# The up projection of a gated MLP by Strassen's seven block products, with the down projection as a stage of its own

## The chip, the core and the metric

The kernel runs on one core of a Trainium2 chip. The metric is device time in microseconds (us) of one execution; several executions are timed and their median is taken. A profile is one more execution, with every instruction recorded on its engine: TensorE (PE, with its weight loads as PEld), VectorE (DVE), ScalarE (ACT), GpSimd (POOL) and SyncE (SP, whose queue issues the DMAs here).

## What is computed

One encoder block: a retention mixer and a Mamba-2 mixer, gated and merged, then an output projection and a conv-gated MLP. 1024 tokens and 16 meta tokens, model width 1024, MLP width 2816. The change touches what follows the mixers:

```python
    merged = jax.nn.sigmoid(gate_ret) * y_ret + jax.nn.sigmoid(gate_ssd) * y_ssd
    h = h + merged @ w_out

    f = dw_conv_centred(rms_norm(h, norm_ffn_w) @ w_ffn_up, w_ffn_conv, b_ffn_conv)
    fg, fu = _split(f, (D_FF, D_FF))
    return h + (jax.nn.silu(fg) * fu) @ w_ffn_down
```

`dw_conv_centred` is a depthwise convolution over three neighbouring tokens. A last `rms_norm` follows and the meta tokens are dropped.

## The kernel before

Activations lie feature-major: 128 features on the partitions, tokens along the free dimension. Every dense product is split so that float32 precision is kept with TensorE's float32r matmuls: an operand x is carried as hi + lo, and a product is hi·hi + hi·lo + lo·hi, three matmuls for each 128 features of the contraction (`mm3`, lines 140 to 142). `wload` (lines 126 to 134) brings 512 KB of weights by DMA into one of two `wraw` buffers, ACT casts them to `whi`, DVE subtracts to get `wlo`; three of each are kept. `fm` makes a block: 8 x 3 matmuls into one bank of PSUM.

The code is written engine-neutral in one order; a scheduler then sets the order of each engine's instructions, and each engine runs its own queue in order.

Output projection (lines 996 to 1013): for each of three token blocks of 342 (`BLK_B`) and each of eight output tiles d, load `w_o[d]`, make the block, add the residual into `h2[d]`, and sum squares into `acc` on POOL. `norm2` turns a finished block into `u2h`, `u2l`, the normalized MLP input in two parts; the last block's `norm2` is called between products of the first feature tile.

MLP (from line 1016): `up_tile(j)` takes feature tile j of 22, which has a gate half and an up half. For each half it loads one weight tile, makes three blocks of 342 tokens, copies them out of PSUM on ACT (line 1033), and runs the convolution: one POOL instruction (line 1039) and two on DVE (lines 1040, 1041) over 1024 tokens. The gate half gets SiLU on ACT; DVE multiplies the halves (line 1065), and the result is split into `ah[j]`, `al[j]` (lines 1068, 1069), which stay in SBUF, six of each. The 22 tiles form six parts of four or three. When a part is done, the next part's first tile is made and then `down` multiplies the finished part with its weights, 512 tokens at a time, and DVE adds the products to `h2` in SBUF (line 1088). The down projection is thus woven into the up projection. `last_down` does the last part in blocks of 256 tokens together with the final norm and the output.

## Time and profile before

| | us |
|---|---|
| device time, median of 3 runs | 2515.85 (2509.86 to 2518.0) |
| span of the profiled execution | 2511.8 |
| PE busy in it | 2423.6 (96%) |
| DVE, ACT, POOL busy | 1179.7 (47%), 770.1 (31%), 671.4 (27%) |
| output projection, from 1660.4 to 1752.1 us | 91.7 |
| MLP without the last part of the down projection, 1752.1 to 2466.0 us | 713.9 |
| last part, 2466.0 to 2499.3 us | 33.3 |

The page gives no other time of the profiled execution than its span, which lies within the three runs and 4.0 us below their median. The rows below come from that execution. A row of a group gives line, engine, operation, output and inputs with their shapes, the count, the busy time, and the mean duration of one in ns; a row of a timeline gives start and duration in us, and in brackets how long the engine had been idle and what ended that. Durations of matmuls that follow each other overlap in such rows, so what one costs is read from the distance between starts.

### The profile page before, as it was taken

The page shows a single profiled execution, that of the slowest core. Times are in us where ns is not written, and L with a number is a line of the kernel's source. Part 1 is how long each engine was busy: PE and PEld are TensorE (multiplying, and loading weights), DVE is VectorE, ACT ScalarE, POOL GpSimd, SP SyncE. Part 2 cuts the span into 40 slices and gives each one's busy share as a digit, 9 for nine tenths or more (in the row PEclk, how much of TensorE's full clock was granted, in tenths as well). Part 3 has the DMA queues.
Part 4 walks back from the last instruction along what each step waited for, and adds up shares of the span by engine and source line. Part 5 has one row for each costly group of instructions (what it writes and reads, how often), then busy time and mean ns, then how long its engine had stood idle before and what let it go on. Part 6 is the DMA issues. An engine that isn't in the chain of part 4 may idle for free.

```text
span 2511.8 us, 36889 instructions
## 1 busy us (share of the span) xinstructions
PE 2423.6 (96%) x15114; PEld 2274.8 (91%) x15114; DVE 1179.7 (47%) x1595; ACT 770.1 (31%) x1345; POOL 671.4 (27%) x763
## 2 busy tenths in 40 slices
PE   7999999999899899989988999999999999999998
PEld 7999999998798889779888999999999989898997
DVE  6243343645634653563374442447543434444356
ACT  4312212333442542343233320235321212121224
POOL 2121221125514633651462122222110101010112
PEclk9999999999899999989999999999999999999999
DMA  4111112124722851572367643345111111111112
GB/s 145 53 47 43 51 47 62 56 80 145 172 72 100 183 115 55 162 169 55 102 192 151 202 141 101 96 134 167 50 51 42 51 44 49 51 43 51 43 43 76
DMA packets 125001, 231.70 MB, mean 92 GB/s; under 512 B 16608, under 2 KB 77536, under 8 KB 120736
## 3 DMA queue, kind: packets, MB, share of 16 engines
q1 hardware_dynamic: 124832, 229.34, 32.0%
q8 instruction: 119, 1.95, 0.3%
q14 instruction: 50, 0.41, 0.1%
HBM read 187.83 MB, written 41.47 MB: 91 GB/s over the span
## 4 chain that ended last, share of the span: by engine, by line
PE 79%; DMA 6%; DVE 5%; POOL 5%; ACT 3%; issue 2%; SPq 0%; DVEq 0%; POOLq 0%; ACTq 0%
PE psd L140 20%; PE psd L142 20%; PE psd L141 20%; PE psw L140 3%; PE psw L142 3%; PE psw L141 3%; DMA br<-row 3%; PE psy L436 2%; POOL t L822 1%; PE pss L397 1%; PE pss L751 1%; PE psb L772 1%; DMA yl<-yb 1%; DVE br L798 1%; DMA ka<-yr 1%
## 5 line engine op out<-in xcount | busy, mean ns | idle before, releaser
L140 PE MATMUL psd<-uh,whi 128*128 128x342 f32 (+3 forms) x1376 | 463.1, 337 | 7.2 <-ACT gs L285 7.2
L133 DVE TENSOR_TENSOR wlo<-wraw,whi 128x1024 fp32r<-128x1024 f32 (+2 forms) x196 | 250.7, 1279 | 453.1 <-ACT whi L132 452.9
L141 PE MATMUL psd<-ul,whi 128*128 128x342 f32 (+3 forms) x1376 | 443.6, 322 | 0.0
L142 PE MATMUL psd<-uh,wlo 128*128 128x342 f32 (+3 forms) x1376 | 443.0, 322 | 0.0
L132 ACT CAST whi<-wraw 128x1024 fp32r<-128x1024 f32 (+2 forms) x196 | 203.6, 1041 | 605.3 <-PE psd L141 398.2
L141 PE MATMUL psd<-u2l,whi 128*128 128x342 f32 x1056 | 337.1, 319 | 0.1
L142 PE MATMUL psd<-u2h,wlo 128*128 128x342 f32 x1056 | 336.2, 319 | 0.0
L140 PE MATMUL psd<-u2h,whi 128*128 128x342 f32 x1056 | 336.0, 318 | 0.0
L140 PEld LDWEIGHTS psd<-uh,whi 128*128 128x128 f32 (+1 forms) x1376 | 261.7, 190 | 16.8 <-issue 7.9
L141 PEld LDWEIGHTS psd<-ul,whi 128*128 128x128 f32 (+1 forms) x1376 | 261.0, 190 | 7.2 <-issue 6.8
L142 PEld LDWEIGHTS psd<-uh,wlo 128*128 128x128 f32 (+1 forms) x1376 | 260.5, 189 | 0.1
L140 PE MATMUL psd<-whi,uh 128*128 128x256 f32 x768 | 234.0, 305 | 0.4 <-ACT uh L213 0.4
L142 PE MATMUL psd<-whi,ul 128*128 128x256 f32 x768 | 217.2, 283 | 3.2 <-POOL ul L215 2.7
L141 PE MATMUL psd<-wlo,uh 128*128 128x256 f32 x768 | 217.2, 283 | 0.0
L1039 POOL TENSOR_SCALAR fo<-fraw,vec 128x1024 f32<-128x1024 f32 x44 | 83.4, 1896 | 471.4 <-ACT fraw L1033 471.4
L141 PEld LDWEIGHTS psd<-u2l,whi 128*128 128x128 f32 x1056 | 198.6, 188 | 0.9 <-DVE u2l L993 0.4
L140 PEld LDWEIGHTS psd<-u2h,whi 128*128 128x128 f32 x1056 | 198.9, 188 | 0.3
L142 PEld LDWEIGHTS psd<-u2h,wlo 128*128 128x128 f32 x1056 | 199.1, 189 | 0.0
L140 PEld LDWEIGHTS psd<-whi,uh 128*128 128x128 f32 x768 | 146.5, 191 | 11.5 <-issue 8.9
L141 PEld LDWEIGHTS psd<-wlo,uh 128*128 128x128 f32 x768 | 147.0, 191 | 5.9 <-issue 5.3
L142 PEld LDWEIGHTS psd<-whi,ul 128*128 128x128 f32 x768 | 146.3, 191 | 4.0 <-POOL ul L215 3.1
L140 PE MATMUL psw<-ah,whi 128*128 128x512 f32 (+1 forms) x400 | 149.1, 373 | 0.0
(239 smaller groups left out, 4628.1 us busy)
## 6 DMA issues: line engine op xcount, KB each, us to landing
br<-row SPq DMA_DIRECT2D x32, 1024.0 KB
wraw<-in_w_up SPq DMA_DIRECT2D x44, 512.0 KB
gt<-gate SPq DMA_DIRECT2D x72, 171.0 KB
wraw<-in_w_xbc SPq DMA_DIRECT2D x24, 512.0 KB
wraw<-in_w_o SPq DMA_DIRECT2D x24, 512.0 KB
wraw<-in_w_dn SPq DMA_DIRECT2D x19, 512.0 KB
gate<-gs SPq DMA_DIRECT2D x48, 171.0 KB
ka<-ys SPq DMA_DIRECT2D x32, 256.5 KB
```

The source lines that it names most:

```text
L132: nc.scalar.copy(hi[:, :n], raw[:, :n])
L133: nc.vector.tensor_sub(lo[:, :n], raw[:, :n], hi[:, :n].bitcast(F32))
L140: nc.tensor.matmul(ps, ah, bh, start=(i == 0), stop=False)
L141: nc.tensor.matmul(ps, ah, bl, start=False, stop=False)
L142: nc.tensor.matmul(ps, al, bh, start=False, stop=(i == n - 1))
L397: nc.tensor.matmul(ps[:, :256], st[("kd", d, c)][:n], vv(c), start=True, stop=True)
L436: nc.tensor.matmul(py[:n, :256], a, b, start=(i == 0), stop=(i == len(mms) - 1))
L751: nc.tensor.matmul(ps, bk(c), st[("xw", d, c)][:n], start=True, stop=True)
L772: nc.tensor.matmul(ps[:n, :], tk("ct", c - 1), st[("pb", c)], start=True, stop=True)
L798: nc.vector.tensor_tensor(r, r, tok[:n, c, 0, g * 16:g * 16 + 16].unsqueeze(2).broadcast_to([n, 16, n]), op=ALU.add)
L822: nc.gpsimd.tensor_tensor(hv(t1[:n]), hv(x), bc(cd[:n, 0:8], n), op=ALU.mult)
L1039: nc.gpsimd.tensor_scalar(o, raw[:, 2:2 + SEQ], V("fconv_w", 3 * f + 1), V("fconv_b", f), op0=ALU.mult, op1=ALU.add)
```

## The change

The up projection of one feature tile has 2 x 2 blocks: W's two halves of the contraction (512 features each) by gate and up half, and u's two halves of the contraction by two sets of tokens. Strassen's form (with Winograd's sums) makes that product from seven block products instead of eight. A block product here is 4 x 3 matmuls of 256 or 258 tokens. Tokens are taken in two rounds (`RND`), 0 to 511 and 512 to 1025, two blocks each.

- `norm2_steps` normalizes a round in place in `hb`, forms four sums and differences of its blocks (t1 to t4; three on POOL, one on DVE), and splits the seven operands `b11`, `t2`, `t1`, `t3`, `b21`, `t4`, `b22` into hi and lo, on ACT and DVE. Both rounds' operands stay in SBUF.
- `weights(j)` loads the gate and the up tile. Four POOL instructions of 512 columns turn the raw tiles into the four weight sums, in place, and ACT and DVE split seven blocks of 512 columns (as `a1`, `a2`, `s24`, `s31`). There are five buffers each for hi and lo, in two pools.
- `up_round` makes the seven products in four PSUM banks: `p2`, `p4` and `p3` accumulate on banks that held another product. Five additions on DVE and two copies on ACT combine them into `f`. All eight banks are used once in a feature tile.
- `conv_steps` is the convolution, now with the multiplication of the halves on POOL. The result goes to DRAM (`act_d`) instead of SBUF.
- The output projection runs in two rounds of 16 weight loads in all (before: three blocks, 24 loads). `h2` is also stored to DRAM (`h2_d`), since `hb` is used for other things in the MLP, and read back for the down projection.
- The down projection follows the last feature tile: `act_load` reads a tile of activations back and splits it on ACT and DVE.

The rest of the kernel is the same. The diff, cut to this; lines that only fell away (the old `norm2`, `up_tile` and their loops) are those of the code above:

```diff
+RND = [((0, 256), 256), ((512, 770), 258)]
+RB = [((0, 256), (256, 256)), ((512, 258), (770, 256))]
...
+    hb = hp.tile([P, KT, NB + 2], F32, name="hb")
...
+    def op_tiles(pool, r):
+        n = RND[r][1]
+        return {o: [pool.tile([P, 4, n], F32R, name=f"{o}{x}{r}", tag=f"{o}{x}") for x in "hl"] for o in OPS}
+    ops = [op_tiles(oa, 0), None]
...
+    def norm2_steps(r, acc):
+        t0 = RB[r][0][0]
+        m = RB[r][0][1] + RB[r][1][1]
+        n = RND[r][1]
+        u = [[hb[:, 4 * k:4 * k + 4, s:s + n] for s in RND[r][0]] for k in range(2)]
+        t1, t3, t2, t4 = u[0][0], u[0][1], u[1][1], u[1][0]
+        def put(o, src):
+            hi, lo = ops[r][o]
+            nc.scalar.copy(hi, src)
+            nc.vector.tensor_sub(lo, src, hi.bitcast(F32))
+        def scale():
+            for b0, bn in RB[r]:
+                ps = pm.tile([P, 512], F32, name="psn", tag="psm")
+                a = acc[:, b0 - t0:b0 - t0 + bn]
+                nc.tensor.matmul(ps[:, :bn], ones, a, start=True, stop=True)
+                nc.scalar.activation(a, ps[:, :bn], AF.Sqrt, bias=eps, scale=1.0 / D)
+                nc.vector.reciprocal(a, a)
+        def first():
+            for d in range(KT):
+                hs = hb[:, d, t0:t0 + m]
+                nc.vector.scalar_tensor_tensor(hs, hs, V("norm_ffn", d), acc[:, :m], op0=ALU.mult, op1=ALU.mult)
+                if d == 3:
+                    put("b11", u[0][0])
+            put("b22", u[1][1])
+            nc.gpsimd.tensor_sub(t1, u[0][1], u[0][0])
+            nc.gpsimd.tensor_sub(t3, u[1][1], u[0][1])
+            nc.vector.tensor_sub(t2, u[1][1], t1)
+            put("t2", t2)
+        def rest():
+            put("t1", t1)
+            put("t3", t3)
+            put("b21", u[1][0])
+            nc.gpsimd.tensor_sub(t4, u[1][0], t2)
+            put("t4", t4)
+        return [scale, first, rest]
...
+    for r in range(2):
+        t0 = RB[r][0][0]
+        m = RB[r][0][1] + RB[r][1][1]
+        acc = sg.tile([P, 516], F32, name="acc", tag="ka", bufs=3)
         for d in range(KT):
             hi, lo = wload(t["w_o"][d])
+            xr = wo.tile([P, 516], F32, name="xr", tag="xr")
+            nc.sync.dma_start(out=xr[:, :m], in_=t["xT"][:, d, T0 + t0:T0 + t0 + m])
+            hs = hb[:, d, t0:t0 + m]
+            for b0, bn in RB[r]:
+                ps = fm(hi, lo, mh, ml, KT, b0, bn)
+                sl = slice(b0 - t0, b0 - t0 + bn)
+                nc.vector.tensor_tensor(hs[:, sl], ps[:, :bn], xr[:, sl], op=ALU.add)
+            nc.sync.dma_start(out=h2_d[:, d, t0:t0 + m], in_=hs)
             if d == 0:
+                nc.scalar.activation(acc[:, :m], hs, AF.Square)
             else:
+                sq = wo.tile([P, 516], F32, name="sq2", tag="sq")
+                nc.scalar.activation(sq[:, :m], hs, AF.Square)
+                nc.gpsimd.tensor_tensor(acc[:, :m], acc[:, :m], sq[:, :m], op=ALU.add)
+            if d in (1, 2, 3) and pend is not None:
+                pend[d - 1]()
+        pend = norm2_steps(r, acc)
...
+    ops[1] = op_tiles(ob, 1)
+    nwt = [0]
+    def wsplit(src, n):
+        pool = wp if nwt[0] % 5 < 3 else wx
+        nwt[0] += 1
+        hi = pool.tile([P, 1024], F32R, name="whi", tag="whi", bufs=3 if pool is wp else 2)
+        lo = pool.tile([P, 1024], F32R, name="wlo", tag="wlo", bufs=3 if pool is wp else 2)
+        nc.scalar.copy(hi[:, :n], src)
+        nc.vector.tensor_sub(lo[:, :n], src, hi[:, :n].bitcast(F32))
+        return hi, lo
+    def weights(j):
+        w = {}
+        def load():
+            w["r"] = r = []
+            for half in range(2):
+                raw = wp.tile([P, 1024], F32, name="wraw", tag="wraw", bufs=2)
+                nc.sync.dma_start(out=raw, in_=t["w_up"][half * NF + j])
+                r.append(raw)
+            w["a1"] = wsplit(r[0], 1024)
+        def sums():
+            r = w["r"]
+            a11, a12, a21, a22 = r[0][:, :512], r[0][:, 512:], r[1][:, :512], r[1][:, 512:]
+            w["a2"] = wsplit(a22, 512)
+            nc.gpsimd.tensor_tensor(a22, a21, a22, op=ALU.add)
+            nc.gpsimd.tensor_sub(a21, a11, a21)
+            nc.gpsimd.tensor_sub(a11, a22, a11)
+            nc.gpsimd.tensor_sub(a12, a12, a11)
+        def s24():
+            w["s24"] = wsplit(w["r"][0], 1024)
+        def s31():
+            w["s31"] = wsplit(w["r"][1], 1024)
+        return w, [load, sums, s24, s31]
+    def product(ps, w, o, r, start):
+        key, half = {"b11": ("a1", 0), "b21": ("a1", 1), "t4": ("a2", 0), "t2": ("s24", 0), "b22": ("s24", 1),
+                     "t3": ("s31", 0), "t1": ("s31", 1)}[o]
+        hi, lo = w[key]
+        xh, xl = ops[r][o]
+        n = RND[r][1]
+        for k in range(4):
+            c = slice(half * 512 + k * P, half * 512 + (k + 1) * P)
+            for i, (a, b) in enumerate(((hi, xh), (hi, xl), (lo, xh))):
+                nc.tensor.matmul(ps[:, :n], a[:, c], b[:, k, :], start=start and k + i == 0, stop=k == 3 and i == 2,
+                                 skip_group_check=True)
+    def up_round(w, f, r):
+        n = RND[r][1]
+        a, b = RND[r][0]
+        m = RB[r][1][1]
+        x = f[0][:, b:b + n]
+        st = {}
+        def bank(pool, tag):
+            return pool.tile([P, 512], F32, name="psu", tag=tag)
+        def p1():
+            st[1] = bank(pm, "psm")
+            product(st[1], w, "b11", r, True)
+            nc.scalar.copy(x, st[1][:, :n])
+        def p6():
+            st[2] = bank(pd, "psd")
+            product(st[2], w, "t2", r, True)
+            nc.vector.tensor_tensor(x, st[2][:, :n], x, op=ALU.add)
+        def p5():
+            st[3] = bank(pd, "psd") if r else bank(pm, "psm")
+            product(st[3], w, "t1", r, True)
+        def p7():
+            st[4] = bank(pm, "psm")
+            product(st[4], w, "t3", r, True)
+            c = f[1][:, b:b + m]
+            nc.vector.tensor_tensor(c, st[4][:, :m], x[:, :m], op=ALU.add)
+            nc.vector.tensor_tensor(c, st[3][:, :m], c, op=ALU.add)
+        def p2():
+            product(st[1], w, "b21", r, False)
+            nc.scalar.copy(f[0][:, a:a + n], st[1][:, :n])
+        def p4():
+            product(st[4], w, "t4", r, False)
+            nc.vector.tensor_tensor(f[1][:, a:a + n], st[4][:, :n], x, op=ALU.add)
+        def p3():
+            product(st[3], w, "b22", r, False)
+            nc.vector.tensor_tensor(x[:, :m], st[3][:, :m], x[:, :m], op=ALU.add)
+        return [p1, p6, p5, p7, p2, p4, p3]
+    def conv_steps(j, f):
+        o = [hb[:, q, 0:SEQ] for q in (3, 4)]
+        def one(half):
+            fi = half * NF + j
+            raw = f[half]
+            nc.gpsimd.memset(raw[:, NB:NB + 1], 0.0)
+            nc.gpsimd.tensor_scalar(o[half], raw[:, 2:2 + SEQ], V("fconv_w", 3 * fi + 1), V("fconv_b", fi), op0=ALU.mult, op1=ALU.add)
+            nc.vector.scalar_tensor_tensor(o[half], raw[:, 1:1 + SEQ], V("fconv_w", 3 * fi), o[half], op0=ALU.mult, op1=ALU.add)
+            nc.vector.scalar_tensor_tensor(o[half], raw[:, 3:3 + SEQ], V("fconv_w", 3 * fi + 2), o[half], op0=ALU.mult, op1=ALU.add)
+            if half == 0:
+                nc.scalar.activation(o[0], o[0], AF.Silu)
+        def fin():
+            nc.gpsimd.tensor_tensor(o[0], o[0], o[1], op=ALU.mult)
+            nc.sync.dma_start(out=act_d[j], in_=o[0])
+        return [lambda: one(0), lambda: one(1), fin]
+    w, prep = weights(0)
+    for f_ in prep:
+        f_()
+    conv = [lambda: None] * 3
+    for j in range(NF):
+        nxt, prep = weights(j + 1) if j + 1 < NF else (None, [lambda: None] * 4)
+        f = [hb[:, q, :] for q in ((0, 1) if j % 2 == 0 else (5, 6))]
+        ra, rb_ = up_round(w, f, 0), up_round(w, f, 1)
+        if j == 0:
+            ra[0]()
+            ra[1]()
+            pend[0]()
+            ra[2]()
+            ra[3]()
+            pend[1]()
+            for p_ in ra[4:]:
+                p_()
+            pend[2]()
+            rb_[0]()
+            rb_[1]()
+        else:
+            for p_ in (ra[0], rb_[0], ra[1], rb_[1]):
+                p_()
+        prep[0]()
+        conv[0]()
+        for q in (2, 3):
+            if j:
+                ra[q]()
+            rb_[q]()
+        prep[1]()
+        conv[1]()
+        for q, g in ((4, prep[2]), (5, prep[3]), (6, conv[2])):
+            if j:
+                ra[q]()
+            rb_[q]()
+            g()
+        w = nxt
+        conv = conv_steps(j, f)
+    ROW = (2, 7, 0, 1, 5, 6, 3, 4)
...
+    def act_load(j):
+        raw = fp.tile([P, SEQ], F32, name="ar", tag="ar", bufs=4)
+        nc.sync.dma_start(out=raw, in_=act_d[j])
+        acth[j] = fp.tile([P, SEQ], F32R, name="ah", tag="ah", bufs=11)
+        actl[j] = fp.tile([P, SEQ], F32R, name="al", tag="al", bufs=11)
+        nc.scalar.copy(acth[j], raw)
+        nc.vector.tensor_sub(actl[j], raw, acth[j].bitcast(F32))
...
-    def down(pi):
+    def down(pi, nxt):
         p0, nk = PARTS[pi]
         for dd in range(4):
             hi, lo = wload(t["w_dn"][4 * pi + dd, :, :2 * nk * P], 2 * nk * P)
+            if dd < len(nxt):
+                act_load(nxt[dd])
...
+    for j in range(PARTS[0][1]):
+        act_load(j)
+    for c_ in conv:
+        c_()
+    for d in range(KT):
+        nc.sync.dma_start(out=hrow[d], in_=h2_d[:, d, 2:2 + SEQ])
+    for pi, (p0, nk) in enumerate(PARTS[:-1]):
+        q0, nq = PARTS[pi + 1]
+        down(pi, list(range(q0, q0 + nq)))
     last_down()
```

The order of instructions on the engines, at three places. First, DVE over one feature tile in the middle of the MLP. Before (`wlo` is the low part of a weight tile, lines 1040 and 1041 the convolution of a half, `al` the low part of the result):

```order
L133 TENSOR_TENSOR wlo_19083<-wraw_19080,whi_19082 128x1024
L1040 SCALAR_TENSOR_TENSOR fo_18889<-fraw_18809,vec_72,fo_18889 128x1024
L1041 SCALAR_TENSOR_TENSOR fo_18889<-fraw_18809,vec_72,fo_18889 128x1024
L133 TENSOR_TENSOR wlo_19178<-wraw_19175,whi_19177 128x1024
L1040 SCALAR_TENSOR_TENSOR fo_18980<-fraw_18900,vec_72,fo_18980 128x1024
L1041 SCALAR_TENSOR_TENSOR fo_18980<-fraw_18900,vec_72,fo_18980 128x1024
L1065 TENSOR_TENSOR fo_18889<-fo_18889,fo_18980 128x1024
L1069 TENSOR_TENSOR al_18986<-fo_18889,ah_18985 128x1024
```

In the changed kernel (line 1079 is the low part of a weight block, a2 of the next feature tile in the first row, then its s24 and s31; lines 1160 and 1164 are the additions of p4 and p3, line 1175 the convolution's first DVE instruction; in brackets the engines whose signals it waits for):

```order
L1079 TENSOR_TENSOR wlo_17836<-wraw_17768,whi_17835 128x512 [waits DMAHW6_49,PE_49,Activation_49]
L1160 TENSOR_TENSOR hb_12744<-psu_17805,hb_12744 128x256 [waits PE_49]
L1160 TENSOR_TENSOR hb_12744<-psu_17820,hb_12744 128x258 [waits PE_49]
L1164 TENSOR_TENSOR hb_12744<-psu_17779,hb_12744 128x256 [waits DVE_49,PE_49]
L1079 TENSOR_TENSOR wlo_17874<-wraw_17766,whi_17873 128x1024 [waits Activation_49]
L1164 TENSOR_TENSOR hb_12744<-psu_17792,hb_12744 128x256 [waits DVE_49,PE_49]
L1175 SCALAR_TENSOR_TENSOR hb_12744<-hb_12744,vec_72 128x1024 [waits Pool_49]
L1079 TENSOR_TENSOR wlo_17904<-wraw_17768,whi_17903 128x1024 [waits Activation_49]
```

And POOL there (lines 1098 to 1101 are the four weight sums, 1174 the convolution's first instruction, 1181 the multiplication):

```order
L1098 TENSOR_TENSOR wraw_17768<-wraw_17768 128x512 [waits DMAHW6_49,DVE_49,Pool_49]
L1099 TENSOR_TENSOR wraw_17768<-wraw_17766,wraw_17768 128x512 [waits DMAHW5_49,Pool_49]
L1100 TENSOR_TENSOR wraw_17766<-wraw_17768,wraw_17766 128x512 [waits Pool_49]
L1101 TENSOR_TENSOR wraw_17766<-wraw_17766 128x512 [waits Pool_49]
L1173 MEMSET hb_12744 128x1 [waits DVE_49]
L1174 TENSOR_SCALAR hb_12744<-hb_12744,vec_72 128x1024
...
L1181 TENSOR_TENSOR hb_12744<-hb_12744 128x1024 [waits Activation_49]
```

The weights of the next feature tile are now made from raw tiles through POOL, and the first of these steps, a2, waits for PE.

Second, PE at the first feature tile, where round 1 has just been normalized (operands end in h0, l0 for round 0 and h1, l1 for round 1; `whi_16723` belongs to the second feature tile):

```order
L1119 MATMUL psu_16691<-b11h1_16524,whi_16542 128x258 [waits Activation_49]
L1119 MATMUL psu_16691<-b11l1_16525,whi_16542 128x258 [waits DVE_49]
...
L1119 MATMUL psu_16740<-t3h1_16530,whi_16558 128x258 [waits Activation_49]
L1119 MATMUL psu_16810<-b11h0_15443,whi_16723 128x256
```

Ahead of these stand the 84 matmuls of the first tile's round 0, and behind them 31 matmuls of the second tile. Before, two blocks of each half stood there to cover the last `norm2`.

Third, DVE at the end of the up projection (`al` is the low part of an activation tile read back; line 1164 the last products' additions, 1175 and 1176 the last convolution):

```order
L1164 TENSOR_TENSOR hb_12744<-psu_21384,hb_12744 128x256 [waits PE_49]
L1176 SCALAR_TENSOR_TENSOR hb_12744<-hb_12744,vec_72 128x1024 [waits DVE_49]
L1175 SCALAR_TENSOR_TENSOR hb_12744<-hb_12744,vec_72 128x1024 [waits Pool_49]
L136 TENSOR_TENSOR wlo_21699<-wraw_21696,whi_21698 128x1024 [waits DMAHW2_49,Activation_49]
L1176 SCALAR_TENSOR_TENSOR hb_12744<-hb_12744,vec_72 128x1024 [waits DVE_49]
L1237 TENSOR_TENSOR al_21520<-ar_21517,ah_21519 128x1024 [waits DMAHW4_49,Activation_49]
L1237 TENSOR_TENSOR al_21526<-ar_21523,ah_21525 128x1024 [waits DMAHW5_49,Activation_49]
L1237 TENSOR_TENSOR al_21532<-ar_21529,ah_21531 128x1024 [waits DMAHW6_49,Activation_49]
L1237 TENSOR_TENSOR al_21538<-ar_21535,ah_21537 128x1024 [waits DMAHW7_49,Activation_49]
```

The first products of the down projection, which had blocks of the up projection ahead of them, now need these four.

## Rows read from the trace of the kernel before

**Rows 1.** Page, busy time of each engine, and granted clock in 40 slices
```profile
PE 2423.6 (96%) x15114; PEld 2274.8 (91%) x15114; DVE 1179.7 (47%) x1595; ACT 770.1 (31%) x1345; POOL 671.4 (27%) x763
PEclk9999999999899999989999999999999999999999
```
**Rows 2.** Stretches: length, busy us (instructions) of PE, PEld, DVE, ACT, POOL, clock, DMA
```profile
1660.40:1752.10 91.70, 91.70 (x580) 91.31 (x580) 59.72 (x82) 42.72 (x65) 23.29 (x19) 1.00 0.54 174
1752.10:2466.00 713.90, 713.76 (x4115) 671.35 (x4114) 312.14 (x299) 174.15 (x257) 92.60 (x92) 1.00 0.14 47
```
**Rows 3.** ACT's timeline, first block copied out in two feature tiles that follow
```profile
2058.24 0.44 ACT L1033 COPY fraw<-psd 128x342 f32<-128x342 f32 x1
...
2080.78 0.44 ACT L1033 COPY fraw<-psd 128x342 f32<-128x342 f32 x1
```
**Rows 4.** PE's timeline: matmuls of 256, then of 512 columns, first and last
```profile
2477.68 0.29 PE L140 MATMUL psw<-ah,whi 128*128 128x256 f32 x1
...
2483.09 0.28 PE L140 MATMUL psw<-ah,whi 128*128 128x256 f32 x1
2434.99 0.40 PE L140 MATMUL psw<-ah,whi 128*128 128x512 f32 x1
...
2444.79 0.40 PE L140 MATMUL psw<-ah,whi 128*128 128x512 f32 x1
```
**Rows 5.** Groups of ACT and DVE, shapes kept apart: count, busy us, mean ns
```profile
L132 ACT CAST whi<-wraw 128x1024 fp32r<-128x1024 f32 x191 | 199.7, 1047 | 596.0 <-PE psd L141 388.9 <-PE psw L141 145.6 <-PE psd L142 35.4
L926 ACT CAST krh<-ka 128x513 fp32r<-128x513 f32 x32 | 19.5, 622 | 43.0 <-DMA ys<-yt 12.6 <-DMA ka<-ys 12.4 <-DMA ka<-yr 10.5
L927 DVE TENSOR_TENSOR krl<-ka,krh 128x513 fp32r<-128x513 f32 x32 | 22.1, 712 | 39.8 <-ACT krh L926 39.7
L1040 DVE SCALAR_TENSOR_TENSOR fo<-fraw,vec,fo 128x1024 f32<-128x1024 f32 x44 | 56.5, 1285 | 48.5 <-POOL fo L1039 47.5 <-POOL fraw L1027 1.0
L1115 DVE TENSOR_TENSOR h<-psw,h 128x256 f32<-128x256 f32 x32 | 12.9, 414 | 2.9 <-PE psw L142 2.7
L991 DVE SCALAR_TENSOR_TENSOR uf<-h,vec,acc 128x342 f32<-128x342 f32 x24 | 13.0, 572 | 0.3
L1098 DVE RECIPROCAL acc<-acc 128x256 f32<-128x256 f32 x4 | 7.0, 1753 | 1.8 <-ACT acc L1097 1.8
L1097 ACT ACTIVATE acc<-psn,eps 128x256 f32<-128x256 f32 x4 | 1.9, 470 | 1.7 <-PE psn L1096 1.7
```
**Rows 6.** POOL by line: duration min/median/max in ns; last row as group
```profile
L744 POOL TENSOR_TENSOR xw<-x,tok x64: 1032/1043/2429, 547.1 to 1311.8; 128x512 f32<-128x512 f32 x60, 16x512 f32<-16x512 f32 x4
L835 POOL TENSOR_TENSOR t<-t,y x32: 1264/1282/1311, 608.1 to 1347.3; 128x512 f32<-128x512 f32 x32
L215 POOL TENSOR_TENSOR ul<-uf,uh 128x1024 fp32r<-128x1024 f32 x1 | 2.5, 2522 | 8.6 <-ACT uh L213 8.6
```
**Rows 7.** Timelines of DVE and POOL, where instructions of both meet, three times
```profile
2395.99 1.23 DVE L133 TENSOR_TENSOR wlo<-wraw,whi 128x1024 fp32r<-128x1024 f32 x1 [2.73 <-ACT whi L132]
2396.41 1.89 POOL L1039 TENSOR_SCALAR fo<-fraw,vec 128x1024 f32<-128x1024 f32 x1 [6.53 <-ACT fraw L1033]
2407.05 0.96 DVE L133 TENSOR_TENSOR wlo<-wraw,whi 128x768 fp32r<-128x768 f32 x1 [6.12 <-ACT whi L132]
2407.46 1.62 POOL L1039 TENSOR_SCALAR fo<-fraw,vec 128x1024 f32<-128x1024 f32 x1 [6.31 <-ACT fraw L1033]
1777.57 3.16 POOL L1039 TENSOR_SCALAR fo<-fraw,vec 128x1024 f32<-128x1024 f32 x1 [1.60 <-ACT fraw L1033]
1778.52 1.22 DVE L133 TENSOR_TENSOR wlo<-wraw,whi 128x1024 fp32r<-128x1024 f32 x1
```
**Rows 8.** PE's longest idle stretch, and PE and clock in stretches behind it
```profile
1371.70 0.65 PE L140 MATMUL psd<-uh,whi 128*128 128x342 f32 x1 [7.19 <-ACT gs L285]
1372.00:1376.00 4.00, 4.00 (x15) 4.00 (x15) 2.16 (x3) 1.62 (x3) 0.00 (x0) 0.50 0.81 256
```
**Rows 9.** A weight load of 512 KB: issue on SP, first use on ACT
```profile
1738.78 0.33 SPq L129 DMA_DIRECT2D wraw<-in_w_o  x1
1742.13 1.05 ACT L132 CAST whi<-wraw 128x1024 fp32r<-128x1024 f32 x1 [1.04 <-DMA wraw<-in_w_o]
```

117 lines of the change are left out of this document (24 added, 93 removed).

## The prediction, made before the changed kernel ran

> **What bounds the kernel now.** I read the page first: PE is busy 96% of the span at an almost always full clock [rows 1]. The table of stretches then shows the two stages that change: in the output projection and in the MLP, PE is busy in practically every microsecond, while DVE is busy 312 of 714 us, ACT 174 and POOL 93, and DMA moves at a share of 0.14 [rows 2]. So the time of this stage is the number of matmuls times the distance between their starts. Two feature tiles that follow each other begin 2080.78 - 2058.24 = 22.54 us apart [rows 3]; at 144 matmuls of 342 columns that is 0.1565 us for one. The change can gain only by fewer PE microseconds, and it can lose at each place where PE must now wait. Those places are searched below: the chain that makes the next tile's weights, the first tile, and the end of the up projection.
>
> **The matmuls of the up projection.** Two rounds of seven products of 12 matmuls make 168 in a tile instead of 144, each of 256 or 258 columns instead of 342. The trace has matmuls of 256 columns, each with a weight load of its own: 45 distances from 2477.68 to 2483.09, 0.1202 each; and of 512 columns: 42 distances from 2434.99 to 2444.79, 0.2333 each [rows 4]. Between 256 and 342 the distance grows by (0.1565 - 0.1202) / 86 = 0.00042 us for a column, so 258 columns cost 0.1210. A tile needs 84 x 0.1202 + 84 x 0.1210 = 20.26 us instead of 22.54: 2.28 less, and 22 tiles give **-50.2 us**. (Columns fall to 7/8, the time only to 0.90, since a part of each matmul doesn't shrink with the columns.) If the distance is off by 0.002, this term moves by 7 us.
>
> The Trainium skill (TensorE: Matmul & The Clock Gate, Back-to-back issue gap) gives an isolated matmul N/2.4 + 2.5 ns, so 109 ns for 256 columns and 145 for 342; by that the gain would be an estimated 22 x (144 x 0.145 - 168 x 0.1095) = 55 us. The trace has 120 and 156, and the measurement decides.
>
> **The output projection.** It becomes 576 matmuls of 256 and 192 of 258 columns, 576 x 0.1202 + 192 x 0.1210 = 92.5 us, instead of 576 of 342, 90.1: **+2.4**. That 8 of 24 weight loads go, and that the sums of squares move to fewer, longer instructions, is worth nothing: PE did not wait there [rows 2].
>
> **The wait in each feature tile.** Before, a tile's weights came ready through one ACT cast and one DVE subtraction, far ahead. Now the order shows a chain. The hi part of a2 of the next tile takes the buffer of the current tile's a1, so ACT waits for the last matmul of `b21` in round 1; call its issue T. Then come: 0.16 to the matmul's end, ACT's cast of 512 columns 0.62, DVE's lo part 0.71 [rows 5], then four POOL sums one after the other. POOL instructions of 512 columns took 1.04 with a second operand that is broadcast and 1.28 with two full ones, and 2.52 at 1024 [rows 6]; I take 1.28, 5.1 in all. Then ACT casts s24, 1.05, and DVE makes its lo part, 1.23: 8.9 in all, some 9.1 with hand-overs. Meanwhile PE has `t4` and `b22` in two rounds, and of the next tile `b11` in two rounds: six products, 72 matmuls, 8.7, then two matmuls of `t2` (hi·hi, hi·lo) before it needs the lo part: 8.9. So PE stands some 0.2 us in each tile if nothing meets the chain. What can meet it are a convolution's POOL instruction (some 1.1 alone) or its DVE instruction, 1.29 [rows 5], and the order puts both near it, so up to 1.3. I take 0.45 in each of 20 tiles, near the lower end since the waits before T leave the queues empty: **+9**; bounds 0 (sums of 1.04) and 26 (1.3 each).
>
> The engines beside the chain are no bound by themselves: in 20.3 us, POOL has 4 x 1.28 + 2 x 1.1 + 2.5 = 9.8 and DVE 3 x 1.23 + 0.71 + 4 x 1.29 = 9.5, beside ten PSUM additions of 0.41 [rows 5], 13.7 in all. The store and the reload of activations and h2 cost nothing on the path: 44 loads and stores of 512 KB in a stretch whose DMA share is 0.14 [rows 2], at 3.35 us from issue to use [rows 9] against 20 us of lead. Without that cover one load would cost those 3.35.
>
> **The first tile.** After the last block of the output projection come the addition 0.41 and the square on ACT, some 0.6, POOL's sum 1.28, the norm's matmul, Sqrt 0.47, two reciprocals of 256 columns, 1.75 each, six scalings of 512 columns (0.57 at 342, so some 0.77 each), two additions of 0.41 and b11's lo part, 1.2 [rows 5, 6]: 12.9. With a weight's lo part that the order puts ahead of the reciprocals, 1.23, and hand-overs, b11 is ready some 14.9 us after the last block. PE has the first tile's round 0, 84 matmuls less what stands ahead of the norm, and is through at about 11.5: it waits 3.4. Then round 1's `t3` needs POOL's t1 and t3, 2.5 each at 1024 elements [rows 6], the lo and hi parts, and comes at 22.5, where PE with b11, part of `t3` and nothing else in its order is through at 16.2: 6.3 more. The norm's matmul itself waits for POOL, 0.8. In sum 10.5. After its longest idle stretch of before, 7.19 us, the granted clock was 0.50, the level of 1.2 GHz, and 4.00 us held only 15 matmuls of 342 columns [rows 8], which at 0.1565 take 2.35: 1.7 lost. **+12.2**; bounds 6 (the waits overlap, full clock) and 18.
>
> **The end of the up projection.** Before, a finished part's `down` had a tile of the next part ahead of it. Now all of DVE's late work stands between the last product and the down projection: p3's addition 0.41, two of the convolution's instructions and one more, 1.29 each, a weight's lo part 1.23, and four lo parts of activations, 1.23 each [rows 5]. Summed, the fourth activation's lo part is ready at 10.4 us, with hand-overs and a POOL instruction in the convolution's chain up to 12.2; I take 11.2. PE's first 48 matmuls of 512 columns use all four; the order lets 20 of them come ahead of the fourth, the other 28 x 0.2333 = 6.5 come after it. Of 11.2 + 6.5 = 17.7 us, 48 x 0.2333 = 11.2 is work: 6.5 lost, with hand-overs 7, and 1.7 for the clock: **+8.7**; bounds 4 and 15.
>
> **The sum.** -50.2 + 2.4 + 9 + 12.2 + 8.7 = -17.9. The profiled execution's 2511.8 us of span becomes 2493.9; that span lies 4.0 below the median of the runs, 2515.85, so the median becomes **2498**.
>
> **Rivals.**
> (a) The covers hold: POOL's sums take 1.04, no instruction meets the chain, the first tile costs 6 and the end 4. -50.2 + 2.4 + 10 = -37.8: 2478. For it: POOL's 60 instructions at 1.04 [rows 6] and the small busy shares [rows 2]. Against: these had a broadcast operand.
> (b) One instruction of 1.1 to 1.3 meets the chain in every tile: +26 in place of +9, 2515, no change that shows. For it: the order puts the convolution's DVE instruction right between s24's and s31's lo parts.
> (c) Slower: DVE and POOL exclude each other. Where DVE's subtraction had begun 0.42 us before, POOL's instruction took 1.89 beside one of 1.23 and 1.62 beside one of 0.96, so it ends some 1.1 after DVE's end in both; beside two, 3.16 [rows 7]. If a POOL instruction of 1.1 and a DVE instruction of 1.29 both come into the chain in every tile, PE waits 2.4 a tile, 21 times: 50 in place of 9, 2539. It turns slower where the wait passes 26.9 / 21 = 1.28 us a tile. Against: during the four sums the order gives DVE mostly additions from PSUM, and POOL's 32 instructions with two full operands all took 1.26 to 1.31 [rows 6].
> The Trainium skill (SBUF — State Buffer, Who interferes with whom) states it as a rule: a DVE instruction with two inputs in SBUF contends with a GpSimd instruction that reads SBUF, and the second to issue blocks until the first is done. It speaks against this change, which gives POOL four sums a tile; the rows agree with it for POOL as the second, and no row shows how often it would strike.
> (d) The change doesn't bring what it says: a matmul of 256 columns, with banks changing and weights of its own, costs more than 0.134 us (22.54 / 168), and the saving is eaten; at 0.140 a tile takes 23.5, 22 x (23.5 - 20.26) = 71 more than in the sum, 2569. Against: the 45 distances of 0.1202, and weight loads there, too [rows 4].
>
> **How the numbers follow.** Forecast (2490 to 2508) 0.47, (a) 0.21, (b) 0.17, (c) 0.12, (d) 0.03. About 0.3%, 7.5 us, is what a measurement of this kernel can tell from no change. Forecast and (a) make faster, 0.68; (b) the same, 0.17; (c) and (d) slower, 0.15. The range reaches from a little below (a), with the first term 4 us better, to half way between (b) and (c): 2474 to 2530.
>
> **What would show it.** Starts of the up projection's matmuls 0.120 apart say the first term is right; 0.134 would kill the gain. Tiles 20.3 to 20.7 apart: the forecast; 21.5: (b); 22.6: (c). In the chain of waits, idle time of PE should end at s24's lo part (line 1079), at b11 and t3 of round 1 in the first tile, and at `al` ahead of the down projection, with a lower clock only behind the last two. The forecast is wrong if PE idles elsewhere, above all at DMA arrivals or at a PSUM bank that an addition has not freed, or if POOL's sums take 2 us or more.

## The result: slower, and where the time went

The changed kernel takes 2535.88 us (median of four runs, 2529.71 to 2537.23) where the kernel before takes 2515.07 in runs beside it: a ratio of 1.0084, 95% interval 1.0066 to 1.0103. It is 0.8% slower, some 21 us, and lies above the forecast (2498) and above its range (2474 to 2530). One execution of a later run, the one with the normalization in seven pieces, was a slow one (4961.14 us) and is left out of that run's time.

The page of the kernel after, busy time of each engine and granted clock in 40 slices, as in [rows 1]:

```profile
PE 2387.7 (94%) x15836; PEld 2230.3 (88%) x15836; DVE 1290.1 (51%) x1822; ACT 771.7 (31%) x1320; POOL 853.9 (34%) x873
PEclk9999999999899999999998999999899999999999
```

PE is busy 36 us less than before, so the change did take work off PE, but the span is 16.1 us longer (2527.9 against 2511.8): 52 us of new idle time. Idle time of PE is where it waits, so the question is where it waits now. Four stretches of the kernel after show in which stages, with the columns of [rows 2]: the output projection, the first two feature tiles, the next twenty, and the down projection up to its last part.

```profile
1658.15:1761.94 103.79, 96.16 (x774) 95.43 (x773) 57.50 (x67) 34.22 (x42) 32.81 (x18) 0.97 0.53 150
1761.94:1823.27 61.33, 44.07 (x296) 41.95 (x295) 44.40 (x45) 20.68 (x28) 24.50 (x19) 0.86 0.20 65
1823.27:2248.72 425.45, 409.04 (x3361) 403.60 (x3359) 269.54 (x362) 116.96 (x178) 230.07 (x179) 1.00 0.22 76
2254.47:2476.87 222.40, 215.50 (x914) 172.66 (x913) 107.38 (x128) 42.86 (x44) 7.72 (x2) 0.98 0.31 109
```

In each of them PE's busy time is now less than the length; before, the two were equal, but for 0.14 us of 714 in the MLP [rows 2]. A tile in which PE never waits takes 20.0 us: in the run without weight sums below, twenty tiles follow each other in 399.95 us, all of it PE time. With that price, and 168 matmuls a tile, so 0.119 each, the account of the two profiled executions is:

| us | measured | predicted |
|---|---|---|
| up projection's matmuls, 22 x (20.0 - 22.54) | -55.9 | -50.2 |
| output projection, 103.8 - 91.7 | +12.1 | +2.4 |
| first two tiles, 61.3 less 288 matmuls (34.3) | +27.0 | +12.2 |
| next twenty tiles, 425.4 - 400.0 | +25.4 | +9 |
| start of the down projection, 222.4 less 912 matmuls (212.8) | +9.6 | +8.7 |
| last part, from its first matmul to the end of the span, 51.0 - 49.5 | +1.5 | 0 |
| waits in the MLP of before that are gone; stages ahead of the change | -1.5; -2.2 | 0 |
| sum | +16 | -17.9 |

The saving came, and a little larger. What was mis-sized is the losses: the next four rows add to 74 us where 32 had been expected. PE's waits of the kernel after from the up projection to the start of the down projection, the four longest rows (what it waited for: us in total, times, longest):

```profile
PE psu L1119 <- ACT whi L1078: 15.4, 10, 5.7
PE psu L1119 <- DVE wlo L1079: 10.2, 15, 0.8
PE psw L143 <- ACT ah L1236: 5.9, 1, 5.9
PE psu L1119 <- ACT t3h L1008: 5.1, 1, 5.1
```

The first two rows are the product t2 with s24 (lines 1078 and 1079 are `wsplit`), the third is the first matmul of the down projection, the fourth round 1 of the first tile. The output projection has three waits of its own, PE's timeline there:

```profile
1732.50 0.39 PE L143 MATMUL psd<-mh,whi 128*128 128x256 f32 x1 [2.01 <-DVE hb L1052]
1744.08 0.48 PE L143 MATMUL psd<-mh,whi 128*128 128x256 f32 x1 [4.05 <-DVE hb L1052]
1750.53 0.39 PE L145 MATMUL psd<-mh,wlo 128*128 128x258 f32 x1 [1.57 <-DVE wlo L136]
```

A wait costs more than its length. The first two stretches below are one in full work and one right behind waits of 0.92 and 0.76 us at t2 in tile 16, followed by two matmuls of the second. The third stretch holds two waits of the same lengths in tile 11, followed by the matmul at which the second of them ended, and the next one:

```profile
2098.00:2104.00 6.00, 6.00 (x52) 6.00 (x51) 2.23 (x3) 1.94 (x3) 5.22 (x4) 1.00 0.23 90
2108.80:2113.00 4.20, 4.11 (x21) 4.11 (x22) 3.10 (x6) 1.14 (x2) 2.10 (x1) 0.59 0.38 125
...
2109.67 0.42 PE L1119 MATMUL psu<-t2l,whi 128*128 128x256 f32 x1
2109.88 0.41 PE L1119 MATMUL psu<-t2h,wlo 128*128 128x256 f32 x1
...
2000.50:2003.00 2.50, 1.21 (x8) 1.01 (x9) 1.99 (x4) 1.72 (x4) 0.61 (x1) 1.00 0.35 139
...
2002.29 0.38 PE L1119 MATMUL psu<-t2h,wlo 128*128 128x256 f32 x1 [0.76 <-DVE wlo L1079]
2002.51 0.28 PE L1119 MATMUL psu<-t2h,whi 128*128 128x256 f32 x1
```

In tile 16 the granted clock is 0.59 behind the waits, and the starts are 0.21 us apart instead of 0.12: the clock had gone to its lower level, 1.2 GHz, for 3.4 us. In tile 11 the granted clock stays 1.00, and only the matmul right behind each wait is slow, with 0.22 us to the next start.

Distances between starts, over their full price, give the shares. In the twenty tiles, distances above 0.45 us (the waits) add 20.1 us, the matmuls right behind a wait 3.6, and the lower clock of tile 16 1.5: together the 25.4 us within 0.2. (The rows of waits count from a matmul's modelled end and give 16.4 in these tiles.) In the first two tiles the lower clock costs 5.8 us, and in the output projection 3.0 beside 8.1 of waits.

### The profile page after: what moved, and what is told of

Read it like the earlier page. It is cut to its first block, busy times and chain, and to the rows that moved or that the text cites. A ratio compares the mean times of both kernels' runs of the same rounds, so it can differ in the third digit from the quotient of the medians.

```text
span 2527.9 us, 38787 instructions
## 1 busy us (share of the span) xinstructions
PE 2387.7 (94%) x15836; PEld 2230.3 (88%) x15836; DVE 1290.1 (51%) x1822; ACT 771.7 (31%) x1320; POOL 853.9 (34%) x873
## 5 line engine op out<-in xcount | busy, mean ns | idle before, releaser
L136 DVE TENSOR_TENSOR wlo<-wraw,whi 128x1024 fp32r<-128x1024 f32 (+1 forms) x144 | 190.5, 1323 | 217.1 <-ACT whi L135 216.8
L135 ACT CAST whi<-wraw 128x1024 fp32r<-128x1024 f32 (+1 forms) x144 | 149.3, 1039 | 482.7 <-PE psd L144 281.6
L1079 DVE TENSOR_TENSOR wlo<-wraw,whi 128x1024 fp32r<-128x1024 f32 x88 | 112.6, 1284 | 113.7 <-ACT whi L1078 113.6
L144 PE MATMUL psw<-al,whi 128*128 128x512 f32 (+1 forms) x400 | 149.0, 373 | 1.0 <-DVE al L1237 1.0
L145 PE MATMUL psw<-ah,wlo 128*128 128x512 f32 (+1 forms) x400 | 146.4, 367 | 0.0
L1078 ACT CAST whi<-wraw 128x1024 fp32r<-128x1024 f32 x88 | 81.5, 940 | 201.4 <-POOL wraw L1101 100.3
L143 PE MATMUL psd<-krh,whi 128*128 128x342 f32 x384 | 123.6, 322 | 3.2 <-ACT krh L932 3.2
L144 PE MATMUL psd<-krl,whi 128*128 128x342 f32 x384 | 123.7, 322 | 0.3 <-DVE krl L933 0.3
L145 PE MATMUL psd<-krh,wlo 128*128 128x342 f32 x384 | 123.4, 322 | 0.0
```

Of the source, the lines that this page charges most:

```text
L135: nc.scalar.copy(hi[:, :n], raw[:, :n])
L136: nc.vector.tensor_sub(lo[:, :n], raw[:, :n], hi[:, :n].bitcast(F32))
L143: nc.tensor.matmul(ps, ah, bh, start=(i == 0), stop=False)
L144: nc.tensor.matmul(ps, ah, bl, start=False, stop=False)
L145: nc.tensor.matmul(ps, al, bh, start=False, stop=(i == n - 1))
L1078: nc.scalar.copy(hi[:, :n], src)
```

## The experiments

Each run is given with its ratio to runs of the kernel before, taken beside it on the same chip; the kernel after stands at 1.0084. The diffs are against the kernel after.

### 1. Is it the chain behind a2, or POOL's sums themselves?

The four sums of tiles 2 to 22 written to free rows of `hb`, so that they need not wait for a2's split, which waits for a1's buffer:

```diff
-            w["a2"] = wsplit(a22, 512)
-            nc.gpsimd.tensor_tensor(a22, a21, a22, op=ALU.add)
-            nc.gpsimd.tensor_sub(a21, a11, a21)
-            nc.gpsimd.tensor_sub(a11, a22, a11)
-            nc.gpsimd.tensor_sub(a12, a12, a11)
+            if j == 0:
+                w["a2"] = wsplit(a22, 512)
+                s31_, s24_ = r[1], r[0]
+            else:
+                s24_, s31_ = hb[:, 2, :1024], hb[:, 7, :1024]
+            w["q"] = s24_, s31_
+            s3, s1, s2, s4 = s31_[:, :512], s31_[:, 512:], s24_[:, :512], s24_[:, 512:]
+            nc.gpsimd.tensor_tensor(s1, a21, a22, op=ALU.add)
+            nc.gpsimd.tensor_sub(s3, a11, a21)
+            nc.gpsimd.tensor_sub(s2, s1, a11)
+            nc.gpsimd.tensor_sub(s4, a12, s2)
+            if j:
+                w["a2"] = wsplit(a22, 512)
...
```

> The four weight sums of tiles 2 to 22 go to two rows of hb that are free by then, so they no longer wait for a2's split, which waits for a1's buffer. Theory 1 (the wait of PE at t2 is the length of the chain from a1's last matmul through a2 and four sums in a row): PE's idle time before the products of t2, 20 us over tiles 3 to 22 and 5.7 in tile 2, falls to under 5 in all, tiles come 20.3 us apart, and the kernel takes 2510 to 2518 us. Rival (DVE and POOL lock each other out, so that the sums cost their time wherever they stand): PE waits as long, 2529 to 2537 us.

Measured: 2503.43 us, ratio 0.9959 (0.9942 to 0.9976), 31 us below the kernel after. Twenty tiles take 403.3 us instead of 425.4, the first two 55.9 instead of 61.3. PE's waits in this run from tile 3 on are one row:

```profile
PE psu L1127 <- DVE hb L1159: 0.9, 3, 0.4
```

Theory 1 holds, and the gain is larger than it said: the tiles are back within 3.4 us of PE's own price, 400.0, and the granted clock is 1.00 in them. The rival falls, though not because DVE and POOL leave each other alone. POOL's timeline of this run, two of the four sums of one tile, and DVE's beside it:

```profile
2016.61 2.28 POOL L1105 TENSOR_TENSOR hb<-wraw 128x512 f32<-128x512 f32 x1
2018.85 2.28 POOL L1106 TENSOR_TENSOR hb<-hb,wraw 128x512 f32<-128x512 f32 x1
...
2015.44 2.29 DVE L1183 SCALAR_TENSOR_TENSOR hb<-hb,vec 128x1024 f32<-128x1024 f32 x1 [1.11 <-POOL hb L1182]
2017.66 2.31 DVE L1184 SCALAR_TENSOR_TENSOR hb<-hb,vec 128x1024 f32<-128x1024 f32 x1
```

The two engines take turns here, and each needs 2.3 us for what takes 1.28 alone, more than in the kernel after. It costs PE next to nothing, because its waits in these tiles are the 0.9 us above.

The sums left out (four lines deleted; s24 and s31 are split from the raw tiles, so other products are computed):

> The four weight sums are left out (s24 and s31 are split straight from the raw tiles; the products are then other ones). Theory 1: what it gains is what the run with spare rows gains, within 4 us, and 3 us more at the first tile, where the sums stand before the first t2: 2507 to 2516. Rival (POOL's work itself is the cost, by blocking DVE): it gains 20 us or more over the run with spare rows, which gains little.

Measured: 2489.47 us, ratio 0.9912 (0.9896 to 0.9929). That is 12 us below the run with spare rows by the ratios, more than theory 1 allowed and less than the rival: twenty tiles take 399.95 instead of 403.3, so the sums themselves cost 3 us there, and the first two tiles 48.7 instead of 55.9, where the sums of tile 1 stand ahead of the first t2 and those of tile 2 between the other work of this place.

The sums on DVE, in place, with the wait on a2 unchanged (`nc.gpsimd` to `nc.vector` in the four lines):

> The changed kernel with its four weight sums on DVE, in place as before, so that they still wait for a2's split and a1's buffer, and only their length changes (POOL 4 times 1.29 and a hand-over of 0.43 us, DVE 4 times 0.69, as seen with sums of the first tiles on DVE). Theory 1 (start plus length of the chain makes the wait at t2): the chain becomes some 2.5 us shorter than PE's cover needs, the idle time at t2 in tiles 3 to 22 falls from 20 to under 4 us, the first tiles win some 3 to 6, and the kernel takes 2507 to 2516. Rival (DVE is the engine that everything waits for, and gets 2.8 us more a tile): idle time goes over to other products, 2520 or more.

Measured: 2506.22 us, ratio 0.9982 (0.9969 to 0.9995). The twenty tiles take 409.0 us; PE's waits in them:

```profile
PE psu L1119 <- DVE wlo L1079: 6.1, 8, 0.8
```

So a shorter chain with the same start gains most of what an earlier start gains; 6.1 us of waits are left where under 4 were expected, and the time is just below what theory 1 gave. Start and length together make the wait at t2, and DVE, busy for 322 of the 409 us, is not short of time in these tiles.

### 2. The output projection

The normalization of round 0 in seven pieces behind output tiles 1 to 7 instead of three behind 1 to 3:

```diff
-            if d in (1, 2, 3) and pend is not None:
+            if d and pend is not None:
...
-        return [scale, first, rest]
+        return [scale, first, rest] if r else [scale, g1, g2, g3, g4, g5, g6]
```

> The normalization of round 0 is cut into seven pieces, put behind output tiles 1 to 7 of round 1 of the output projection instead of three behind tiles 1 to 3. Theory 1 (DVE's additions, which free PE's banks, queue behind 20 us of DVE work in three places): PE's idle time in this stage falls from 7.6 us to under 2, the stage from 103.8 to 94 or 95 us, the kernel to 2525 to 2529. Rival (the stage is long for its matmuls and its DMA, or DVE is slowed by POOL in any order): the stage stays above 101 us, 2533 to 2538.

Measured: the stage 97.9 us (103.8), PE's waits there 3.4 us (7.6). Theory 1 names the cause but not all of it. The whole time, 2529.24 us, ratio 1.0066 (1.0047 to 1.0085), is not clear of the kernel after: in the profiled execution the stages ahead take 2.8 us longer, and PE then waits 5.3 us instead of 3.6 for the first t2. What is left is a second cause. POOL's timeline in this run, then DVE's:

```profile
1731.87 2.39 POOL L1033 TENSOR_TENSOR hb<-hb 128x1024 f32<-128x1024 f32 x1 [4.08 <-DVE b11l L1009]
1734.22 1.75 POOL L1082 TENSOR_TENSOR acc<-acc,sq 128x514 f32<-128x514 f32 x1
...
1732.06 4.46 DVE L1022 SCALAR_TENSOR_TENSOR hb<-hb,vec,acc 128x512 f32<-128x512 f32 x2
1736.44 1.21 DVE L136 TENSOR_TENSOR wlo<-wraw,whi 128x1024 fp32r<-128x1024 f32 x1
```

Two scalings that take 0.74 us each elsewhere took 4.46 together: the first lasted until 0.55 us after the end of POOL's difference t1 (line 1033), the second until 0.55 after the end of POOL's next sum, and the weight's lo part, for which PE waits, stands behind them. So the differences were moved to DVE as well (lines 1026, 1027 and 1035, `nc.gpsimd` to `nc.vector`):

> As the run with the normalization in seven pieces, and the differences t1, t3 and t4 are made on DVE instead of POOL. Theory 2 (of what is left in the output projection, most is DVE blocked by POOL's instructions of 1024 elements, seen as subtractions that take 2.3 to 3.3 us instead of 1.2): the stage falls from 97.9 us to 95 or less and the kernel to 2523 to 2527, though DVE gets 3.7 us more work. Rival (DVE has too much work in this stage): the stage grows to 99 us or more, 2531 to 2536.

Measured: the stage 96.8 us, between the two theories; the whole time 2521.59 us, a little below theory 2; ratio 1.0049 (1.0028 to 1.0071). The rival falls, since more work on DVE did not lengthen the stage. Of theory 2 the larger part showed up behind the stage: from the start of the up projection to t4 of tile 2 it is 58.6 us instead of 62.9. What still stands in the stage are 2.4 us of waits for DVE and 1.5 of the lower clock.

### 3. The first tiles

The raw weights of tile 1 loaded right behind the last `w_o` tile:

> The two raw weight tiles of the first feature tile are loaded right behind the last tile of the output projection, ahead of its residual and its stores. Theory 1 (the first t2 waits for its loads): PE's idle time before the first t2 falls from 3.6 us to under 1.5, the kernel to 2530 to 2534. Rival (the four sums on POOL, in a row and between other work, set that time): 3 us or more are left, 2533 to 2538.

Measured: 2532.16 us, ratio 1.0078 (1.0061 to 1.0096), and PE waits 3.7 us before the first t2, as before. The time lies in the range of theory 1, but it is not clear of the kernel after, and the wait decides: the loads are not the cause; with the run without sums, in which this wait is gone, it is the four sums in a row.

Sums of the first two tiles and differences t1, t3, t4 on DVE and b21 ahead of t2 in round 1, on top of spare rows, seven pieces, buffers on the left (below) and the early load. First these four edits alone:

> Spare rows for the sums, the normalization in seven pieces, the buffers on the left and the early loads together. If the waits are in separate places, the gains add: 32 + 6 + 3 + 2 us from 2536, so 2491 to 2498. If what is gained in one place is waited for in the next (an earlier end of the output projection lets PE only wait longer in the first feature tile), 2498 to 2505.

Measured: 2495.93 us, ratio 0.9931 (0.9907 to 0.9954). The gains add as forecast, so the places are mostly separate. Then with the first tile:

> The four edits, and in the first feature tile the differences t1, t3, t4 and the weight sums of the first two tiles on DVE, and in round 1 the product of b21 (which needs no sum) ahead of that of t2. Theory 2 (POOL's 2.4 us for 1024 elements and its lock with DVE make the chain ahead of round 1 long): from the start of the up projection to t4 of the second tile 45 to 48 us instead of 56 to 61, and the kernel 6 to 10 us below the four edits alone. Rival (reciprocals and scalings on DVE alone set it, and DVE gets more work): within 3 us of the four edits.

Measured: 2489.48 us, ratio 0.9911 (0.9896 to 0.9925), and 51.2 us from the start of the up projection to t4 of tile 2 (58.7 with the four edits). The kernel is 6 us better, as theory 2 said, though the stretch is 3 us longer than it said. This version is 0.9% faster than the kernel before. PE still waits 5 us at the first matmul of t3 in round 1, while b21 is ready: the scheduler put that one matmul ahead of it. So t3 was made ahead of b21 (the diff's lines in `first`):

```diff
...
+            put("b22", u[1][1])
+            nc.vector.tensor_sub(t1, u[0][1], u[0][0])
+            nc.vector.tensor_sub(t3, u[1][1], u[0][1])
+            put("t3", t3)
+            put("b21", u[1][0])
...
```

> As the run with the first feature tile reworked, with t3 of round 1 made and split ahead of b21, t2 and t1, since one matmul of t3 stands first in PE's order there. If that matmul holds up 30 others that are ready: its wait falls from 5.0 us to 2.5 to 3.5, and the kernel comes 2 to 3 us below the run it is made from, 2486 to 2488. If what follows is late anyway: the wait moves to the next product, within 1 us of it.

Measured: 2491.68 us, ratio 0.9915 (0.9899 to 0.9932), no difference. PE's timeline of this run has the wait where it was:

```profile
1779.67 0.58 PE L1163 MATMUL psu<-t3h,whi 128*128 128x258 f32 x1 [4.60 <-ACT t3h L1008]
```

On DVE, b22's lo part still came ahead of the difference t3, and a wait of 0.85 us at t2 followed. Neither theory's number fits. The order of the run before shows that the one matmul holds up ready ones: b21's parts were there 3.4 us before it started. That moving it pays was not shown.

### 4. The start of the down projection

The buffers of the activations that are read back, over operands that are done with earlier:

```diff
+    ap = fp_es.enter_context(tc.tile_pool(name="ap", bufs=1, reuse_waits="tile"))
...
-        raw = fp.tile([P, SEQ], F32, name="ar", tag="ar", bufs=4)
+        raw = ap.tile([P, SEQ], F32, name="ar", tag="ar", bufs=4)
```

> The buffers of the activations that are read back lie over round 0's operands, which are done with earlier, instead of over operands of the last products. Theory 1 (PE's 5.9 us behind the last product are a wait for loads that are issued only after it): that idle time falls below 3 us and the kernel to 2530 to 2533. Rival (as predicted, DVE's queue of convolution and lo parts sets the time): the first matmul comes earlier, but the fourth lo part as late as before, and the down projection starts its steady run within 1.5 us of before: 2534 to 2537.

Measured: 2528.73 us, ratio 1.0068 (1.0051 to 1.0085), the down projection 220.9 us instead of 222.4. PE's first wait falls from 5.9 to 2.8 us, and 2.4 us come back two rows later at the first lo part (1.0 before). So theory 1 is right on the first wait and the rival on the stage, which is 1.5 us shorter; the whole time is below both and not clear of the kernel after. DVE's timeline behind the last product, which ended at 2258.19:

```profile
2262.52 1.28 DVE L1175 SCALAR_TENSOR_TENSOR hb<-hb,vec 128x1024 f32<-128x1024 f32 x1 [1.10 <-POOL hb L1174]
2263.72 2.35 DVE L1238 TENSOR_TENSOR al<-ar,ah 128x1024 fp32r<-128x1024 f32 x2
2265.99 1.28 DVE L1176 SCALAR_TENSOR_TENSOR hb<-hb,vec 128x1024 f32<-128x1024 f32 x1
2267.19 2.35 DVE L1238 TENSOR_TENSOR al<-ar,ah 128x1024 fp32r<-128x1024 f32 x2
```

The fourth lo part ends 11.4 us behind the last product's end, the predicted 11.2. To see whether DVE's queue alone sets this, the last tile's convolution was left out as well, on top of these buffers:

> As the run with the buffers on the left, and the convolution of the last feature tile is left out (its activation stored raw), which takes four DVE instructions of 1.28 us out from between the last product and the lo parts of the activations. If DVE's queue sets the start of the down projection, as predicted: the fourth lo part comes some 3 to 5 us earlier and the down projection takes 215 to 218 us instead of 220.9. If the loads set it (SP issues them late, each needs 1.3 us of DMA): 219 us or more.

Measured: 2532.47 us, ratio 1.0086 (1.0064 to 1.0107), the down projection 223.3 us. ACT's timeline of this run:

```profile
2250.32 1.05 ACT L135 CAST whi<-wraw 128x1024 fp32r<-128x1024 f32 x1 [2.38 <-PE psu L1119]
2258.12 1.04 ACT L135 CAST whi<-wraw 128x1024 fp32r<-128x1024 f32 x1 [6.75 <-DMA wraw<-in_w_dn]
2260.64 1.04 ACT L1237 CAST ah<-ar 128x1024 fp32r<-128x1024 f32 x1 [1.47 <-DMA ar<-act]
2261.90 1.04 ACT L1237 CAST ah<-ar 128x1024 fp32r<-128x1024 f32 x1 [0.22 <-DMA ar<-act]
```

The last product ends at 2253.11 here, and the first cast of a load comes 7.5 us behind it; with the convolution in place it came 1.9 us behind. SP's order changed with the edit: three more reads of h2 now stand ahead of the four loads, which are issued 0.6 us before the last product's end instead of 4.4. So in this run the loads set the start, and in the run before, where ACT had made the fourth hi part by 2264.93 and DVE its lo part by 2269.54, DVE's queue did. What the convolution costs by itself was not measured, and what either limit would leave without the other stays open.

## Why the prediction failed, step by step

The profiled execution is 34 us above the forecast's sum. By size, the terms that failed are the wait in each feature tile (16.4 us more than its term), the first tile (14.8) and the output projection (9.7); the matmuls give 5.7 back.

- **What bounds the kernel, the up projection's matmuls:** right. A tile has 7/8 of the block products, and they came at 0.119 us a matmul, 5.7 us better than summed. That a matmul of 256 columns would eat the saving (rival d) is refuted.
- **The output projection: the step that failed first in time.** It was costed as matmuls alone, +2.4 us, with "PE did not wait there" from the kernel before [rows 2]. But the change puts a whole round's normalization, with its sums and seven splits, into DVE's queue of this very stage, in three lumps. It measured +12.1, and the sign that the prediction had named itself, a PSUM bank that an addition has not freed. DVE's timeline between two of PE's waits, first and last rows, and POOL's beside the first:

```profile
1732.70 3.07 DVE L136 TENSOR_TENSOR wlo<-wraw,whi 128x1024 fp32r<-128x1024 f32 x1
1735.69 2.33 DVE L1009 TENSOR_TENSOR b22l<-hb,b22h 128x1024 fp32r<-128x1024 f32 x1
...
1742.48 1.22 DVE L1009 TENSOR_TENSOR t2l<-hb,t2h 128x1024 fp32r<-128x1024 f32 x1
1743.61 1.08 DVE L1052 TENSOR_TENSOR hb<-psd,xr 128x258 f32<-128x258 f32 x3
...
1732.25 2.43 POOL L1027 TENSOR_TENSOR hb<-hb 128x1024 f32<-128x1024 f32 x1 [0.69 <-DVE hb L1022]
```

  For 11 us DVE works on splits and a sum; then come three additions at once (line 1052), for which PE's banks had waited. It is not the amount of work: DVE is busy 57.5 us in this stage, and 59.7 before [rows 2]. It is that the pieces come in one lump, two of them lengthened by POOL, ahead of the additions: the run with seven pieces took 5.9 us off the stage. Nothing of this was costed: what is queued behind the moved work on its engine was asked for the MLP only.
- **The first tile:** 27.0 us against 12.2 and an upper bound of 18. The waits that were named came: 5.1 at t3 (6.3 forecast), 1.5 at b11 (3.4), 1.0 at the norm (0.8). The lower clock, put at 1.7, cost 5.8. Two waits were not named, both at t2, where the first tiles have the same chain of sums as all others but less work of other tiles to cover it:

```profile
1767.09 0.39 PE L1119 MATMUL psu<-t2h,whi 128*128 128x256 f32 x1 [3.56 <-ACT whi L1078]
...
1812.97 0.58 PE L1119 MATMUL psu<-t2h,whi 128*128 128x256 f32 x1 [5.65 <-ACT whi L1078]
```

- **The wait in each tile:** the chain that the prediction names is the right one, its size is not. The tiles came 21.3 us apart, 25.4 us in all, where 9 was taken and 26 was the upper bound and the price of rival (b). Chain and cover were worked out as 9.1 and 8.9 us; measured, from ACT's cast of a2 to the end of s24's lo part, the chain takes 9.2 us in a tile in which nothing meets it, with 0.56 us of wait, and 10.8 us in the tile below, with 2.0. ACT's cast of a2, POOL's multiplication of the halves and its last two sums, DVE, and the two matmuls that wait:

```profile
1991.45 0.62 ACT L1078 CAST whi<-wraw 128x512 fp32r<-128x512 f32 x1 [0.65 <-ACT hb L1156]
...
1990.63 2.40 POOL L1181 TENSOR_TENSOR hb<-hb 128x1024 f32<-128x1024 f32 x1 [4.01 <-ACT hb L1178]
...
1996.38 1.29 POOL L1100 TENSOR_TENSOR wraw<-wraw 128x512 f32<-128x512 f32 x1
1997.74 2.16 POOL L1101 TENSOR_TENSOR wraw<-wraw 128x512 f32<-128x512 f32 x1
...
1992.10 1.47 DVE L1079 TENSOR_TENSOR wlo<-wraw,whi 128x512 fp32r<-128x512 f32 x1 [1.07 <-ACT whi L1078]
...
1997.41 1.34 DVE L1079 TENSOR_TENSOR wlo<-wraw,whi 128x1024 fp32r<-128x1024 f32 x1 [2.58 <-ACT whi L1078]
2001.01 1.23 DVE L1079 TENSOR_TENSOR wlo<-wraw,whi 128x1024 fp32r<-128x1024 f32 x1 [2.26 <-ACT whi L1078]
...
2001.03 0.38 PE L1119 MATMUL psu<-t2h,whi 128*128 128x256 f32 x1 [0.92 <-ACT whi L1078]
2002.29 0.38 PE L1119 MATMUL psu<-t2h,wlo 128*128 128x256 f32 x1 [0.76 <-DVE wlo L1079]
```

  DVE and POOL meet twice here. a2's lo part came while POOL was multiplying the halves (line 1181) and took 1.47 us instead of 0.69. s31's lo part had begun on DVE just ahead of the fourth sum, which took 2.16 us instead of 1.29. Over the twenty tiles the fourth sum loses 7 us in this way, in eight tiles, and a2's lo part 5.9 us in the eleven tiles that have a meeting and a wait. This is the lock, the rival (c). Fifteen tiles wait 20.1 us in all; at 0.56 each, with nothing in the way, it would be 8.4, so the lock makes some 11 to 12 us where 50 had been its price. The taken 0.45 was argued from "the waits before T leave the queues empty"; with a cover 0.2 us shorter than the chain there was no room for any meeting, and the upper bound was the value to take.

  The prediction has a2 wait for a1's last matmul in every tile. In every fifth one (5, 10, 15, 20) ACT's cast of a2 begins 2.3 us before that matmul ends, and PE does not wait, though the chain is the longest there, 11.0 us. Why the cast may begin earlier stays open; but these tiles show, within the kernel itself, that the start of the chain decides.
- **The end of the up projection:** right within 1 us (9.6 against 8.7), with the fourth lo part 12.5 us behind the last product (12.2 as the upper end). But a part of the mechanism was missed, so the fit is in part luck. SP's timeline, and ACT's first cast:

```profile
2249.69 5.30 SPq L132 DMA_DIRECT2D wraw<-in_w_dn  x2
2255.09 1.92 SPq L1233 DMA_DIRECT2D ar<-act  x4
...
2259.46 1.04 ACT L1236 CAST ah<-ar 128x1024 fp32r<-128x1024 f32 x1 [3.87 <-DMA ar<-act]
```

  The loads were to cost nothing, with "20 us of lead"; but they stand behind a weight load on SP that waits for its buffer, and are issued 0.6 us after the last product.
- **The profile explains 16 us; the medians differ by 21.** The profiled execution is the fastest of the four runs. What the others lose more was not shown. Why DVE's additions of squares in the last part (line 1291) take 549 ns on average, where they took 491, stays open.

## What to carry over

A chain that is a few tenths shorter or longer than its cover must be costed at its upper bound. An earlier start is the best cure (spare rows won 31 us), and a shorter chain wins most of it (the sums on DVE won 26). Work that is moved into a stage must be laid out in the queues of that stage, engine by engine, also where that stage had no waits at all before: ask which instruction PE waits for next stands behind it. A lock between two engines is worth what its place is worth; the run with spare rows has more of it and is faster.
